# One tile of x moved to GpSimd's queue, and a scratch of its own for the squares, in the opening of an encoder layer

## The chip, the core and the metric

The kernel runs on one core of a Trainium2 chip. A core has five engines that each run their own instruction stream in order: TensorE (PE: matrix products and transposes), VectorE (DVE), ScalarE (ACT), GpSimd (POOL) and SyncE (SP). They wait for one another through semaphores. Transfers between device memory and the on-chip memory are issued by SP, ACT or POOL and carried by 16 DMA engines. The metric is the device time of one execution in microseconds; smaller is better. In this text a "queue" with a q (ACTq, SPq, POOLq) is the part of an engine that issues transfers and handles waits.

## The reference

One layer of a hybrid encoder on 512 positions of width 2048. Cut to what the opening of the kernel computes:

```python
c_act = jax.nn.silu(c)                                # c: one row of 2048
mod = c_act @ w_ada + b_ada                           # 2048 x 6144
shift, scale, gate = jnp.split(mod, 3, axis=-1)
h = rms_norm(x, g) * (1.0 + scale[:, None]) + shift[:, None]
proj = jnp.einsum('bsd,df->bsf', h, w_in)             # 512 x 7168
# attention over three dilated windows and two-way retention on slices of proj,
# gated by silu(z), then
out = jnp.einsum('bsf,fd->bsd', y, w_out)
return x + gate[:, None] * out                        # and a final rms_norm
```

All is float32. The kernel computes each product of two float32 matrices as three products of rounded parts (high by high, high by low, low by high), so that every weight is first split into a high part (ACT) and a low part (DVE).

## The kernel before

**Tiling.** The 512 positions are four tiles of 128 rows (`xn[0]` to `xn[3]`, named `xt` in the profile), each 128 x 2048. The 2048 columns are 16 blocks of 128 (`k`). `h` is kept transposed, one 128 x 512 tile for each block `k`: `hh[k]` the high part, `hl[k]` the low part.

**Two parts of the program.** The projections go over the blocks in chunks of 1, 2, 2, 3, 4 and 4 blocks (`CHUNKS`), because the shift and scale of a block can only be had after a sum over all 2048 rows of `w_ada`. While the matrix products of one chunk run, DVE adds up the rows of `w_ada` for the next (`ada_pieces`: tile `araw` for the raw rows, `aacc` for the sum, three buffers of `araw`, `AR = 3`). The first chunk is block 0 alone, and nothing runs under which its shift and scale could be hidden. It is made in a **prelude** in which TensorE does the sums itself. The prelude is the place of the change. It ends where the first product `pw<-hh,whi` of the projections starts; then come the chunks, the heads and the output projection, which the change leaves as they are.

**The prelude, in the order in which it is written.** For each tile `t` of x: `squares_a(t)` sums the squares of the left half on ACT (tile `sqa`, of which only the sum is used), `squares(t)` those of the right half on DVE (`sqd`); `factor(t)` makes the sum `ms` on DVE and its inverse root `rsx` on POOL; `scaled(t, ...)` multiplies the tile on DVE; `k0_part(t)` and `turned(t, b)` transpose its blocks on PE into `psk` and `psx`; `evacuated(t, b, act)` copies them out on ACT. Between these lie, on PE, `warm(n, ...)` (products whose result is not used, two instructions each), the sums of block 0 `sums0(b, i)` over four transfers `raw0` of `w_ada` (`b`: shift or scale, `i`: upper or lower half of the rows; 512 KB each in pieces of 512 bytes) and `turn_rows()`, which turns the biases and the gain (`bg_row`). `silu_c` makes `ct`, the factors of those sums, from `c_row`.

**What sets the order.** Instructions written through `pin(...)` stay in program order on their engine; the others are placed by a scheduler at build time. An engine's stream is in order at run time: an instruction that waits holds all that stand behind it. Each transfer from SP or ACT is given one of eight completion semaphores in turn (`DMAHW0` to `DMAHW7` in the order listings); the ninth such transfer is issued only after the one that had its semaphore before has landed. Transfers from POOL have semaphores of their own (`DMASW0`, `DMASW1`, ...). Of the prelude's, ACT issues five (four of x, and `raw_w`, the first weights of `w_in`), SP the rest.

**Buffers.** `sqa` is taken from the three buffers of `araw`, so the first three transfers of `araw` have to wait until the squares that use their buffer are done. The prelude's own pool (`xp`) is closed at the end of the prelude, and its room is used again.

Of the kernel before, what the change touches and what calls it, by code (L numbers as in the profile page):

```python
# [9 lines left out]
F32 = mybir.dt.float32  # L10
F32R = mybir.dt.float32r
I32 = mybir.dt.int32
AF = mybir.ActivationFunctionType
# [4 lines left out]
P = 128  # L18
D = 2048
# [13 lines left out]
OFF_QA, OFF_KA, OFF_VA, OFF_ZA = 0, 1024, 2048, 3072  # L33
OFF_QR, OFF_KR, OFF_VR, OFF_ZR = 4096, 4608, 5120, 6144
UC = 256
# [2 lines left out]
ADA_SPAN = 0.65  # L38
TAB_SPAN = 16
WARM = 9, 2, 8, 6, 4  # L40
FIRST_W = OFF_KA + UC
LAG = 3
RAW, RAW1, WB, LOOK, LEAD, LEAD1, EB, YB = 3, 3, 3, 2, 4, 8, 1, 22
GR = 2
# [2 lines left out]
AR = 3  # L47
# [3 lines left out]
def trunk_kernel(ctx, tc, x, c, norm_gain, w_ada, b_ada, w_in, w_out, dec_f, dec_b, final_gain, out):  # L51
    nc = tc.nc
    x2, o2 = x[0], out[0]
    wi, wo, wa = w_in[0], w_out[0], w_ada[0]
# [23 lines left out]
    def raw_tile():  # L78
        early["n"] += 1
        if early["on"] and early["n"] % 2 == 0:  # L80
            return aap.tile([P, 1024], F32, tag="raw1", name="raw1", bufs=RAW1)
        return wp.tile([P, 1024], F32, tag="raw", name="raw", bufs=RAW)
# [12 lines left out]
    c_row = const.tile([NK, P], F32, name="c_row")  # L95
# [9 lines left out]
    aap = xn_scope.enter_context(tc.tile_pool(name="aap", bufs=2, side="right"))  # L105
    x3p = xn_scope.enter_context(tc.tile_pool(name="x3p", bufs=1, side="right"))
    x_scope = ExitStack()
    xp = x_scope.enter_context(tc.tile_pool(name="xp", bufs=1, side="right"))
# [3 lines left out]
    bg_row = const.tile([48, P], F32, name="bg_row")  # L112
    raw0 = [xp.tile([P, NK, P], F32, name=f"raw0{b}") for b in range(2)]
    xn = [(x3p if t == 3 else xp).tile([P, D], F32, name=f"xt{t}") for t in range(NT)]

    def load0(q, b, i):
        q.dma_start(
            raw0[b][:, i * 8 : (i + 1) * 8],
            wa[i * 8 * P : (i + 1) * 8 * P, b * D : b * D + P].rearrange("(a p) f -> p a f", p=P),
        )  # L120

    for q, t, a, b in ((nc.scalar, 0, 0, 1024), (nc.sync, 0, 1024, D), (nc.scalar, 1, 0, D), (nc.scalar, 2, 0, D), (nc.scalar, 3, 0, D)):
        q.dma_start(xn[t][:, a:b], x2[t * P : (t + 1) * P, a:b])
    nc.gpsimd.dma_start(c_row, c.rearrange("b (k p) -> (b k) p", p=P))
    load0(nc.sync, 0, 0)
    load0(nc.sync, 1, 0)

    raw_w = raw_tile()
    nc.scalar.dma_start(raw_w[:, : 2 * UC], wi[0:P, FIRST_W : FIRST_W + 2 * UC])
    load0(nc.sync, 0, 1)  # L130
    load0(nc.sync, 1, 1)
    nc.gpsimd.dma_start(bg_row[0:32, :], b_ada[:, 0 : 2 * D].rearrange("b (k p) -> (b k) p", p=P))
    nc.gpsimd.dma_start(bg_row[32:48, :], norm_gain.rearrange("b (k p) -> (b k) p", p=P))
    ssx = const.tile([P, NT, 2], F32, name="ssx")
    rsx = const.tile([P, NT], F32, name="rsx")

# [6 lines left out]
    nc.gpsimd.memset(mhalf, -0.5)  # L143
    mln2 = const.tile([P, 1], F32, name="mln2")
    nc.gpsimd.memset(mln2, -math.log(2.0))

    ct = const.tile([P, NK], F32, name="ct")
    ce = const.tile([P, NK], F32, name="ce")
# [5 lines left out]
    pin = tc.keep_in_program_order  # L154
    marks = {}
# [155 lines left out]


    def squares_a(t):
        sa = aap.tile([P, 2048], F32, tag="araw", name="sqa", bufs=AR)
        marks["sq"] = pin(nc.scalar.activation(sa[:, 0:1024], xn[t][:, 0:1024], AF.Square, accum_out=ssx[:, t, 0:1]))

    def squares(t):
        sd = aap.tile([P, 1024], F32, tag="aacc", name="sqd")
# [61 lines left out]
    A, B = slice(0, 3 * P), slice(3 * P, S)  # L380
    warm(WARM[0], psk3)
    squares_a(0)
    squares(0)
    factor(0)
# [14 lines left out]
    sums0(0, 0)  # L399
    turn_rows()  # L400
    squares_a(1)
    squares(1)
    factor(1)
# [10 lines left out]
    turned(1, 3)  # L414
    sums0(0, 1)
    squares_a(2)
    squares(2)
    factor(2)
# [122 lines left out]
    def conv(src, n):  # L541
        hi = wp.tile([P, 512], F32R, tag="whi", name="whi", bufs=WB)
        lo = wp.tile([P, 512], F32R, tag="wlo", name="wlo", bufs=WB)
        dh, dl = hi[:, :n], lo[:, :n]
        if len(src.shape) == 3:
            dh = dh.rearrange("p (k f) -> p k f", k=src.shape[1])
            dl = dl.rearrange("p (k f) -> p k f", k=src.shape[1])
        c1 = nc.scalar.copy(dh, src)  # L548
        c2 = nc.vector.tensor_tensor(dl, src, f32(dh), op=ALU.subtract)  # L549
        marks["conv"] = marks.get("conv", 0) + 1  # L550
        if marks["conv"] == 1:
            after(c1, marks["conv1"][0])
            after(c2, marks["conv1"][1])
        elif marks["conv"] < 4:
            after(c1, marks["hh"])
            after(c2, marks["hl"])
        return hi, lo


    def shared_conv(c0s, k0, nk):  # L560
        m = len(c0s)
        lo_c = min(c0s)
        st = {}

        def ld():
            if k0 == 0 and lo_c == FIRST_W:
                assert m == 2
                st["raw"] = raw_w[:, : 2 * UC].rearrange("p (k f) -> p k f", k=1)
            if "raw" not in st:
                raw = raw_tile()  # L570
                rv = raw[:, : nk * m * UC].rearrange("p (k f) -> p k f", k=nk)
                nc.sync.dma_start(
                    rv,
                    wi[k0 * P : (k0 + nk) * P, lo_c : lo_c + m * UC].rearrange("(k p) f -> p k f", p=P),
                )
                st["raw"] = rv

        def cv(j):
            off = (c0s[j] - lo_c) // UC
            if nk == 1:  # L580
                if off // 2 not in st:
                    a, b = off // 2 * 512, min(off // 2 * 512 + 512, m * UC)
                    st[off // 2] = conv(st["raw"][:, 0, a:b], b - a)
                w = st[off // 2]
                o = off % 2 * UC
                return w[0][:, o : o + UC], w[1][:, o : o + UC]
            return conv(st["raw"][:, :, off * UC : (off + 1) * UC], nk * UC)

        return [(ld, lambda j=j: cv(j)) for j in range(m)]
# [310 lines left out]
    k0 = 0  # L900
# [423 lines left out]
```

## Time and profile before

| | us |
|---|---|
| median of 3 runs | 987.12 (985.5 to 988.26) |
| the profiled execution | 985.0 |
| its span, first to last instruction | 983.2 |
| start of the first product of the projections in it | 50.06 |

The profiled execution lies 1.8 us over its span and 2.1 us under the median. Times in the views count from the start of the span. A timeline row gives start, duration, engine, line and operation, and in brackets how long the engine had been idle before and what released it; a row with xN stands for N instructions. A waits row gives total idle time, how often, and the longest. "DMA to landing" is the time from issue to completion of a transfer.

### The profile page before, as it was taken

What the parts mean: (1) busy time and instruction counts of PE and PEld (TensorE: products, weight loads), DVE (VectorE), ACT (ScalarE), POOL (GpSimd) and SP (SyncE); (2) the same over time, 40 slices, a digit from 0 to 9 for tenths busy, and PEclk for the clock granted to TensorE, in tenths of its full rate; (3) what the DMA queues carried; (4) which work ended last, traced back from release to release, by engine and by line L of the source; (5) the groups of instructions that cost most, each with busy time, mean ns of one, the idle gap of its engine ahead of it and who ended that gap; (6) DMA issues with size and microseconds to landing.
All of it is one profiled execution on the core that took longest, in us unless ns stands there. A gap on an engine that the chain in (4) does not pass through costs nothing.

```text
span 983.2 us, 14429 instructions
## 1 busy us (share of the span) xinstructions
PE 948.1 (96%) x5624; PEld 824.5 (84%) x5624; DVE 613.9 (62%) x1076; ACT 376.3 (38%) x738; POOL 12.3 (1%) x25
## 2 busy tenths in 40 slices
PE   3799999999999999999999999999999999999996
PEld 3588688788988888897998899998899988888896
DVE  1499999976968686665655556745534473535444
ACT  1384243425236454454443232432233362323321
POOL 1000000000000000000000000000000000000001
PEclk7899999999999999999999999999999999999998
DMA  9478879733472222222224624526322248234304
GB/s 327 130 256 289 280 233 339 249 125 108 141 224 86 65 65 64 66 65 80 71 65 139 204 87 153 170 65 203 118 65 87 65 154 296 86 110 147 108 1 171
DMA packets 108947, 141.49 MB, mean 144 GB/s; under 512 B 5656, under 2 KB 78024, under 8 KB 108496
## 3 DMA queue, kind: packets, MB, share of 16 engines
q1 hardware_dynamic: 106912, 134.52, 42.2%
q10 hardware_dynamic: 1872, 6.03, 1.6%
q8 instruction: 44, 0.72, 0.3%
q14 instruction: 23, 0.19, 0.1%
q0 software_dynamic: 96, 0.03, 0.0%
HBM read 136.36 MB, written 4.20 MB: 143 GB/s over the span
## 4 chain that ended last, share of the span: by engine, by line
PE 87%; DMA 5%; DVE 4%; issue 2%; ACT 1%; POOL 0%; SPq 0%; POOLq 0%; DVEq 0%; ACTq 0%
PE pp L92 24%; PE pw L92 14%; PE pp L90 12%; PE po L92 12%; PE pw L90 7%; PE po L90 6%; PE op L92 3%; PE sp L92 2%; DMA graw<-in_w_ada_dram 2%; DMA raw<-in_w_ada_dram 2%; PE op L90 2%; PE tp L783 1%; DVE aacc L214 1%; PE sp L90 1%; DMA araw<-in_w_ada_dram 1%
## 5 line engine op out<-in xcount | busy, mean ns | idle before, releaser
L548 ACT CAST whi<-raw 128x512 fp32r<-128x512 f32 (+1 forms) x289 | 175.3, 607 | 432.4 <-PE pp L92 200.9
L549 DVE TENSOR_TENSOR wlo<-raw,whi 128x512 fp32r<-128x512 f32 (+1 forms) x289 | 193.7, 670 | 209.1 <-ACT whi L548 204.7
L92 PE MATMUL pp<-wlo,hh 128*128 128x256 f32 x576 | 161.8, 281 | 0.6 <-DVE wlo L549 0.6
L90 PE MATMUL pp<-whi,hh 128*128 128x256 f32 x576 | 162.3, 282 | 0.0
L92 PE MATMUL pp<-whi,hl 128*128 128x256 f32 x576 | 161.3, 280 | 0.0
L90 PEld LDWEIGHTS pp<-whi,hh 128*128 128x128 f32 x576 | 108.4, 188 | 2.5 <-ACT sc L852 1.7
L92 PEld LDWEIGHTS pp<-wlo,hh 128*128 128x128 f32 x576 | 108.4, 188 | 1.7 <-DVE wlo L549 0.8
L92 PEld LDWEIGHTS pp<-whi,hl 128*128 128x128 f32 x576 | 108.4, 188 | 0.0
L90 PE MATMUL pw<-hh,whi 128*128 128x512 f32 x256 | 102.6, 401 | 1.8 <-DVE acc L955 1.6
L90 PE MATMUL pp<-hh,whi 128*128 128x512 f32 x256 | 102.0, 398 | 0.4 <-DVE kl L683 0.4
L92 PE MATMUL pw<-hh,wlo 128*128 128x512 f32 x256 | 101.4, 397 | 0.0
L92 PE MATMUL pp<-hh,wlo 128*128 128x512 f32 x256 | 101.3, 396 | 0.0
L92 PE MATMUL pw<-hl,whi 128*128 128x512 f32 x256 | 101.1, 395 | 0.0
L92 PE MATMUL pp<-hl,whi 128*128 128x512 f32 x256 | 100.9, 394 | 0.0
L92 PE MATMUL po<-wlo,yh 128*128 128x512 f32 (+1 forms) x252 | 92.6, 367 | 0.0
L92 PE MATMUL po<-whi,yl 128*128 128x512 f32 (+1 forms) x252 | 92.5, 367 | 0.0
L90 PE MATMUL po<-whi,yh 128*128 128x512 f32 (+1 forms) x252 | 92.5, 367 | 0.0
L214 DVE SCALAR_TENSOR_TENSOR aacc<-araw,ct,aacc 128x512 f32<-128x512 f32 (+2 forms) x75 | 76.0, 1013 | 3.6 <-DMA araw<-in_w_ada_dram 2.3
L955 DVE TENSOR_TENSOR acc<-acc,pw 128x512 f32<-128x512 f32 x100 | 66.7, 680 | 8.0 <-PE pw L92 7.5
L1008 DVE SCALAR_TENSOR_TENSOR gacc<-graw,ct,gacc 128x512 f32<-128x512 f32 x60 | 44.9, 749 | 38.5 <-DMA graw<-in_w_ada_dram 38.1
L90 PEld LDWEIGHTS pw<-hh,whi 128*128 128x128 f32 x256 | 48.1, 188 | 16.3 <-DVE acc L955 4.1
L90 PEld LDWEIGHTS pp<-hh,whi 128*128 128x128 f32 x256 | 48.1, 188 | 13.4 <-ACT e L728 0.9
(233 smaller groups left out, 1567.9 us busy)
## 6 DMA issues: line engine op xcount, KB each, us to landing
raw<-in_w_in_dram SPq DMA_DIRECT2D x94, 512.0 KB, 3.7
araw<-in_w_ada_dram SPq DMA_DIRECT2D x48, 512.0 KB, 6.0
graw<-in_w_ada_dram SPq DMA_DIRECT2D x64, 256.0 KB, 2.9
raw<-in_w_out_dram SPq DMA_DIRECT2D x32, 512.0 KB, 3.7
raw<-in_w_in_dram SPq DMA_DIRECT2D x16, 384.0 KB, 3.7
araw<-in_w_ada_dram SPq DMA_DIRECT2D x16, 384.0 KB, 4.8
res<-in_x_dram SPq DMA_DIRECT2D x16, 256.0 KB, 6.7
xt<-in_x_dram ACTq DMA_DIRECT2D x3, 1024.0 KB, 8.1
```

What stands on the lines that cost most here:

```text
L90: nc.tensor.matmul(o, lh, rh, start=start, stop=False, skip_group_check=True)
L92: nc.tensor.matmul(o, a, b, start=False, stop=stop and b is (rl if swap else rh), skip_group_check=True)
L214: ins = nc.vector.scalar_tensor_tensor(acc[:, :, :n], rv[:, a], ct[:, kr + a : kr + a + 1], acc[:, :, :n], op0=ALU.mult, op1=ALU.add,)
L548: c1 = nc.scalar.copy(dh, src)
L549: c2 = nc.vector.tensor_tensor(dl, src, f32(dh), op=ALU.subtract)
L783: nc.tensor.transpose(tp_[:, j * P : (j + 1) * P], pt[:, j * P : (j + 1) * P], ident)
L955: nc.vector.tensor_tensor(accs[u][i], accs[u][i], ps[i], op=ALU.add)
L1008: nc.vector.scalar_tensor_tensor(st["acc"], raw, ct[:, kr : kr + 1], st["acc"], op0=ALU.mult, op1=ALU.add)
```

## The change

Four edits in the prelude:

1. The tile `xn[1]` is issued by POOL, not by ACT. `c_row` stays ahead of it on POOL; the two transfers of `bg_row` go behind POOL's constants.
2. The early transfer `raw_w` on ACT is gone, and with it the special case that used it. These weights are now loaded as all the others are, by SP, behind the four `raw0`.
3. So eight transfers of the prelude are left on SP and ACT (two halves of `xn[0]`, `xn[2]`, `xn[3]`, four `raw0`).
4. `sqa` is a tile of its own in the prelude's pool.

```diff
-FIRST_W = OFF_KA + UC
...
-    for q, t, a, b in ((nc.scalar, 0, 0, 1024), (nc.sync, 0, 1024, D), (nc.scalar, 1, 0, D), (nc.scalar, 2, 0, D), (nc.scalar, 3, 0, D)):
+    nc.gpsimd.dma_start(c_row, c.rearrange("b (k p) -> (b k) p", p=P))
+    for q, t, a, b in ((nc.scalar, 0, 0, 1024), (nc.sync, 0, 1024, D), (nc.gpsimd, 1, 0, D), (nc.scalar, 2, 0, D), (nc.scalar, 3, 0, D)):
         q.dma_start(xn[t][:, a:b], x2[t * P : (t + 1) * P, a:b])
-    nc.gpsimd.dma_start(c_row, c.rearrange("b (k p) -> (b k) p", p=P))
-    load0(nc.sync, 0, 0)
-    load0(nc.sync, 1, 0)
-
-    raw_w = raw_tile()
-    nc.scalar.dma_start(raw_w[:, : 2 * UC], wi[0:P, FIRST_W : FIRST_W + 2 * UC])
-    load0(nc.sync, 0, 1)
-    load0(nc.sync, 1, 1)
-    nc.gpsimd.dma_start(bg_row[0:32, :], b_ada[:, 0 : 2 * D].rearrange("b (k p) -> (b k) p", p=P))
-    nc.gpsimd.dma_start(bg_row[32:48, :], norm_gain.rearrange("b (k p) -> (b k) p", p=P))
+    for i in range(2):
+        for b in range(2):
+            load0(nc.sync, b, i)
...
     nc.gpsimd.memset(mln2, -math.log(2.0))
+
+    nc.gpsimd.dma_start(bg_row[0:32, :], b_ada[:, 0 : 2 * D].rearrange("b (k p) -> (b k) p", p=P))
+    nc.gpsimd.dma_start(bg_row[32:48, :], norm_gain.rearrange("b (k p) -> (b k) p", p=P))
...
     def squares_a(t):
-        sa = aap.tile([P, 2048], F32, tag="araw", name="sqa", bufs=AR)
-        marks["sq"] = pin(nc.scalar.activation(sa[:, 0:1024], xn[t][:, 0:1024], AF.Square, accum_out=ssx[:, t, 0:1]))
+        sa = xp.tile([P, 1024], F32, tag="sqa", name="sqa")
+        marks["sq"] = pin(nc.scalar.activation(sa, xn[t][:, 0:1024], AF.Square, accum_out=ssx[:, t, 0:1]))
...
         def ld():
-            if k0 == 0 and lo_c == FIRST_W:
-                assert m == 2
-                st["raw"] = raw_w[:, : 2 * UC].rearrange("p (k f) -> p k f", k=1)
             if "raw" not in st:
```

How the built program's streams change, at the three places that the prediction speaks of. The semaphore that an instruction waits for stands in brackets; numbers behind a tile's name are buffer numbers, and the change moves the lines by four to seven.

First ACT, from its first transfer to the first copy of transposed blocks. Before:

```order
L123 DMA xt_110<-in_x_dram 128x1024
L123 DMA xt_111<-in_x_dram 128x2048
L123 DMA xt_112<-in_x_dram 128x2048
L123 DMA xt_113<-in_x_dram 128x2048 [waits DMAHW0_49]
L129 DMA raw<-in_w_in_dram 128x512 [waits DMAHW4_49]
L315 ACT_TABLE_LOAD
L315 ACTIVATE sqa,ssx<-xt_110 128x1024
L280 ACTIVATE ce<-ps_149 128x16 [waits PE_49]
L358 COPY xT_93<-psx 128x2x128 [waits PE_49]
```

Now, as far as the squares of the second tile of x:

```order
L123 DMA xt_110<-in_x_dram 128x1024
L123 DMA xt_112<-in_x_dram 128x2048
L123 DMA xt_113<-in_x_dram 128x2048
L311 ACT_TABLE_LOAD
L311 ACTIVATE sqa,ssx<-xt_110 128x1024 [waits DMAHW0_49]
L276 ACTIVATE ce<-ps_147 128x16 [waits PE_49]
L354 COPY xT_93<-psx 128x2x128 [waits PE_49]
L354 COPY xT_94<-psx 128x2x128
L354 COPY xT_95<-psx 128x3x128 [waits PE_49]
L354 COPY xT_96<-psx 128x4x128 [waits PE_49]
L354 COPY xT_97<-psx 128x4x128 [waits PE_49]
L311 ACTIVATE sqa,ssx<-xt_111 128x1024 [waits DMASW1_49,Activation_49]
```

The two transfers that waited for a semaphore are gone from ahead of ACT's table load and squares, and the second tile's squares wait for a semaphore of POOL's transfers.

Then SP, behind the four `raw0` of the prelude. Before:

```order
L117 DMA raw_109<-in_w_ada_dram 128x8x128
L572 DMA raw_385<-in_w_in_dram 128x768 [waits DMAHW1_49]
L572 DMA raw_389<-in_w_in_dram 128x768 [waits DMAHW2_49]
L572 DMA raw_393<-in_w_in_dram 128x256 [waits DMAHW3_49]
L572 DMA raw<-in_w_in_dram 128x768 [waits DMAHW5_49]
L572 DMA raw<-in_w_in_dram 128x256 [waits DMAHW6_49]
L203 DMA araw<-in_w_ada_dram 128x4x256 [waits DMAHW7_49,Activation_49]
L203 DMA araw<-in_w_ada_dram 128x4x256 [waits DMAHW0_49]
L203 DMA araw<-in_w_ada_dram 128x4x256 [waits DMAHW1_49,Activation_49]
L203 DMA araw<-in_w_ada_dram 128x4x256 [waits DMAHW2_49]
L203 DMA araw<-in_w_ada_dram 128x4x256 [waits DMAHW3_49,Activation_49]
```

Now:

```order
L116 DMA raw_109<-in_w_ada_dram 128x8x128
L565 DMA raw<-in_w_in_dram 128x512 [waits DMAHW0_49]
L565 DMA raw_385<-in_w_in_dram 128x768 [waits DMAHW1_49]
L565 DMA raw<-in_w_in_dram 128x768 [waits DMAHW2_49]
L565 DMA raw_389<-in_w_in_dram 128x768 [waits DMAHW3_49]
L565 DMA raw<-in_w_in_dram 128x256 [waits DMAHW4_49]
L565 DMA raw_393<-in_w_in_dram 128x256 [waits DMAHW5_49]
L199 DMA araw<-in_w_ada_dram 128x4x256 [waits DMAHW6_49]
L199 DMA araw<-in_w_ada_dram 128x4x256 [waits DMAHW7_49]
L199 DMA araw<-in_w_ada_dram 128x4x256 [waits DMAHW0_49]
L199 DMA araw<-in_w_ada_dram 128x4x256 [waits DMAHW1_49]
L199 DMA araw<-in_w_ada_dram 128x4x256 [waits DMAHW2_49]
```

The transfer of the first weights (128x512) is new on SP, and the transfers of `araw` no longer wait for ACT.

Last, ACT at the end of the second chunk, where the scheduler places things differently although nothing was edited there (`junk` is the scratch of the sums that give the next chunk's shift and scale, `aacc<-araw` the first step of the sum for the chunk after it). Before:

```order
L548 CAST whi<-raw 128x512 [waits DVE_49,PE_49]
L548 CAST whi<-raw_636 128x512 [waits DMAHW2_49,DVE_49,PE_49]
L210 ACTIVATE aacc<-araw,ct 128x2x384 [waits DMAHW2_49,DMAHW1_49]
L247 ACTIVATE junk,md<-psm 128x128 [waits PE_49]
L247 ACTIVATE junk,md<-psm 128x128
L247 ACTIVATE junk,md<-psm 128x128 [waits PE_49,Activation_49]
L247 ACTIVATE junk,md<-psm 128x128 [waits Activation_49]
```

Now:

```order
L544 CAST whi<-raw 128x512 [waits DVE_49,PE_49]
L243 ACTIVATE junk,md<-psm 128x128 [waits PE_49]
L243 ACTIVATE junk,md<-psm 128x128
L206 ACTIVATE aacc<-araw,ct 128x2x384 [waits DMAHW1_49,DMAHW0_49]
L243 ACTIVATE junk,md<-psm 128x128 [waits PE_49,Activation_49]
L243 ACTIVATE junk,md<-psm 128x128 [waits Activation_49]
L544 CAST whi<-raw_636 128x512 [waits DMAHW3_49,DVE_49,PE_49]
```

Two of the sums stand ahead of the step that waits for a transfer, and a split of weights stands behind it all. On PE the transposes `psm` that feed these sums stand 16 products earlier, and DVE and SP shift a few instructions by one or two places to match.

## The prediction

> **What bounds the kernel now.** I read the page's slices first, then the waits of the first 50 us, then the timeline there. Of section 2 one row matters here, the rate of all transfers in slices of 24.6 us:
>
> ```profile
> GB/s 327 130 256 289 280 233 339 249 125 108 141 224 86 65 65 64 66 65 80 71 65 139 204 87 153 170 65 203 118 65 87 65 154 296 86 110 147 108 1 171
> ```
>
> In the first slice the transfers run at 327 GB/s, in the second, still in the prelude, at 130: something holds them back. The waits of the first 50 us, ACT's and DVE's, and SP's own, name it:
>
> ```profile
> ACT L315 <- DMA raw<-in_w_ada_dram: 17.5, 1, 17.5
> DVE ms L325 <- ACT sqa L315: 14.8, 2, 13.1
> ```
>
> ```profile
> SPq L203 <- ACT sqa L315: 21.0, 3, 8.0
> ```
>
> ACT does nothing for 17.5 us and then is released by a transfer of `w_ada` that it does not read. DVE waits 13.1 us of that for ACT's squares. SP waits 21.0 us for the squares before it issues three loads of `araw`. The timeline shows how the prelude hangs on it:
>
> ```profile
> 0.74 5.47 ACTq L123 DMA_DIRECT2D xt<-in_x_dram  x4
> ...
> 5.68 1.23 DVE L320 CUSTOM_DVE_ANT_0 sqd<-xt 128x1024 f32<-128x1024 f32 x1 [4.80 <-DMA xt<-in_x_dram]
> ...
> 17.18 0.33 ACTq L129 DMA_DIRECT2D raw<-in_w_in_dram  x1
> 17.54 1.28 ACT L315 ACT_TABLE_LOAD   x1 [17.54 <-DMA raw<-in_w_ada_dram]
> 18.84 1.06 ACT L315 ACTIVATE sqa<-xt 128x1024 f32<-128x1024 f32 x1
> 19.80 0.19 ACT L315 ACTIVATION_READ_ACCUMULATOR sqa<-xt 128x1 f32 x1
> ...
> 20.02 0.16 DVE L325 SCALAR_TENSOR_TENSOR ms<-ssx 128x1 f32<-128x1 f32 x1 [13.11 <-ACT sqa L315]
> ...
> 21.87 3.12 PE L347 MATMUL psx<-ident,xt 128*128 128x128 f32 x15
> ...
> 24.82 1.95 PE L378 MATMUL psk<-ident,ones 128*128 128x128 f32 x16
> ...
> 26.70 1.91 PE L296 MATMUL psa<-raw,ct 128*1 128x128 f32 x16
> 28.54 0.26 PE L272 MATMUL ps<-ident,bg_row 48*128 48x48 f32 x1
> 28.84 0.21 DVE L273 COPY bg<-ps 128x48 f32<-128x48 f32 x1 [5.79 <-PE ps L272]
> ...
> 29.16 1.22 DVE L320 CUSTOM_DVE_ANT_0 sqd<-xt 128x1024 f32<-128x1024 f32 x1
> ...
> 32.35 1.73 PE L347 MATMUL psx<-ident,xt 128*128 128x128 f32 x7 [0.21 <-DVE xt L333]
> ...
> 34.01 3.57 PE L296 MATMUL psa<-raw,ct 128*1 128x128 f32 x16
> ...
> 46.33 0.61 ACT L548 CAST whi<-raw 128x512 fp32r<-128x512 f32 x1
> ...
> 49.84 0.73 ACT L210 ACTIVATE aacc<-araw,ct 128x512 f32<-128x512 f32 x1
> ...
> 50.06 0.48 PE L90 MATMUL pw<-hh,whi 128*128 128x512 f32 x1
> ```
>
> ACT issues four loads of x, then the fifth, `raw_w`, at 17.18: it is a ninth or later transfer and stands until an earlier one gives its semaphore back. Behind it stand the table load and the squares, though half of the first tile was there at 5.68 for DVE. From the squares on the prelude is one chain on PE, ACT and DVE, from 18.84 to 50.06.
>
> **The change part by part.** *ACT is free.* With eight transfers on SP and ACT none of ACT's three has to wait. The squares wait for their data alone. When that is there, a narrow window of ACT's timeline tells, for the fourth load of x waited for the first one's semaphore:
>
> ```profile
> 5.88 0.33 ACTq L123 DMA_DIRECT2D xt<-in_x_dram  x1
> ```
>
> So the first half tile has landed by 5.88; the table load (1.28) fits ahead of that. Squares and their readout took from 18.84 to 19.99, 1.15 us: they end at 7.03 instead, just behind DVE's half (6.91). From there to the first sums on PE (26.70) it was 6.71 us of scaling, transposes and warming products; PE would be ready for the sums at 13.74, a gain of 12.96. That is the most that this edit alone can give there.
>
> *What ends last then.* The sums read the first block of `raw0`, issued by SP. Its issue, and the landings of that line (three have a record):
>
> ```profile
> 1.19 0.42 SPq L117 DMA_DIRECT2D raw<-in_w_ada_dram  x1
> ```
>
> ```profile
> DMA to landing us min/median/max: 14.2/15.4/16.7
> ```
>
> The first block lands at 1.19 + 14.2 = 15.39. It is late because the blocks share the DMA engines with x; the queues between 6 and 10 us (packets, MB; q10 is ACT's, q1 SP's, q0 POOL's):
>
> ```profile
> q10 hardware_dynamic: 194, 1.46, 90.9%
> q1 hardware_dynamic: 195, 0.10, 8.8%
> q0 software_dynamic: 87, 0.03, 3.0%
> ```
>
> The queues take turns packet by packet: 194 against 195, but ACT's are of 8 KB (a row of x) and SP's of 512 bytes. So the block gets through only when x is done. The change leaves the bytes of x the same; a third queue takes turns from SP, but x is through no later. I keep 15.39. The bounds: 13.74, where it does not bind, and 17.15, where the second block lands now, if the third queue pushes the first one back by a block:
>
> ```profile
> 1.66 15.49 DMA raw<-in_w_ada_dram
> ```
>
> So the sums start at 15.39 instead of 26.70: **11.3 us** earlier, with bounds of 13.0 and 9.5.
>
> *The rest of the prelude keeps its length.* Behind the sums stands `turn_rows` on PE, behind it the bias copy on DVE, behind that the right half's squares of the second tile (29.16, now 17.85). These need what POOL issues:
>
> ```profile
> 1.26 0.67 POOL L124 DMA_DIRECT2D c_row<-in_c_dram  x1 [0.82 <-POOLq L1313]
> ```
>
> ```profile
> c_row<-in_c_dram POOLq DMA_DIRECT2D x1, 8.0 KB, 5.8
> bg_row<-in_b_ada_dram POOLq DMA_DIRECT2D x1, 16.0 KB, 6.2
> bg_row<-in_norm_gain_dram POOLq DMA_DIRECT2D x1, 8.0 KB, 6.4
> ```
>
> The second tile is issued at 1.93. No row has a megabyte on this queue. From below: 5.8 us as `c_row`, and 1.05 MB at the 1.59 MB in 4 us (397 GB/s) that all queues had together, 2.6 us: 10.4. From above: the same start and a third of that rate, 7.9 us: 15.7. I take 13, since 8 KB packets take turns with ACT's of the same size, half the rate (5.3 us). All lie ahead of 17.85, so the move costs nothing; without that cover each us past it costs one. `bg_row` follows on that queue: 6.4 us from an issue at some 4, or right behind the tile, so by about 16, needed at 28.54 - 11.3 = 17.24. On ACT the wait for the second tile holds the copies of its own transposes, on PE its transposes: both need that tile anyhow. The issue itself, some 0.7 us on POOL as `c_row`'s, trades places with the two of `bg_row`, and POOL's first root is not due before 7.2.
>
> *The first weights move to SP*, behind `raw0`: an issue at about 15.3, up to 2 us of issue, and a landing within about 6.3 us (the median of line L572 to 60 us is 6.2):
>
> ```profile
> DMA to landing us min/median/max: 6.1/6.2/6.3
> ```
>
> That is about 24; their first use at 46.33 becomes 35.0. Hidden. *The scratch of its own* takes SP's 21.0 us of waiting away. The first sum over `araw`, at 49.84, becomes due at 38.5. By 49.2 us the kernel before had moved 24.6 x (327 + 130) = 11.2 MB; at 327 GB/s that takes 34.4 us. The transfers just keep ahead. With the old scratch the third load would have moved with the squares, so this edit is worth nothing alone here, but guards the rest.
>
> *The clock.* The same 16 sums took 1.91 us at 26.70 and 3.57 at 34.01, and the granted clock differs (1.00 and 0.50, the third figure from the right in these rows of two stretches, ahead of the DMA share and the rate):
>
> ```profile
> 26.00:28.00 2.00, 2.00 (x19) 1.59 (x19) 0.00 (x0) 0.66 (x2) 0.00 (x0) 1.00 0.15 8
> 34.00:36.00 2.00, 2.00 (x11) 1.21 (x11) 0.17 (x2) 1.64 (x4) 0.09 (x1) 0.50 0.03 8
> ```
>
> Which stretch falls to half clock may differ after the move; one such group is 1.66 us, either way. I add nothing to the sum and this much to the range. [...]
>
> *After the prelude.* The chunks are bound by DVE, PE and loads that wait for a buffer of `araw`, not by the rate of the transfers: the two long pieces of transfer in the chain, and the rate in two stretches around them,
>
> ```profile
> 86.05 3.73 DMA araw<-in_w_ada_dram
> ...
> 114.55 6.80 DMA araw<-in_w_ada_dram
> ```
>
> ```profile
> 75.00:80.00 5.00, 5.00 (x36) 4.62 (x35) 4.86 (x8) 1.28 (x3) 0.00 (x0) 1.00 1.07 372
> 100.00:110.00 10.00, 10.00 (x45) 8.03 (x44) 10.00 (x15) 1.94 (x4) 0.00 (x0) 1.00 0.70 231
> ```
>
> 231 GB/s before the longer piece, where 372 were to be had: these loads start late, they aren't starved, and so they move with the rest. The scheduler's new order at the second chunk's end puts 16 products less ahead of the transposes `psm`. If their input is late, PE stands still for as long as these products take, at most: by the 45 products in the 10 us of the second row, 16 x 0.22 = 3.6 us. If it isn't, two sums on ACT no longer stand behind the 3.73 us piece. I take nothing, with 2 us either way.
>
> **The sum.** 985.0 - 11.3 = 973.7 us for a profiled execution. The runs' median is 2.1 above that execution, so 987.12 - 11.3 = **975.8 us**.
>
> **The rivals.**
>
> *The gain is half lost.* POOL's tile or `bg_row` lands at 18 to 25 instead of 13, or the new order costs its 3.6 us. For it: each of POOL's tiny transfers took about 6 us. Against: 87 of their 96 packets ran within the 4 us of that row. Price: gain of 3 to 9, 978 to 984.
>
> *More is gained.* The first block lands by 13.74 and the cold stretch at 34.01 runs at full clock: 13.0 + 1.7, and 0.9, half of the 1.73 of the transposes at 32.35: up to 15.6, so 971.5 to 974. Against: nothing moves bytes of x out of the way.
>
> *Only issue time is saved.* [...] As a mechanism here: two of ACT's issues go, 0.33 us each as at 5.88 and 17.18, and its wait reappears at another transfer: 987.12 - 0.7 = 986.4. Against it, in the timeline: between 6.21 and 17.18 ACT issued nothing at all, and now no transfer of ACT waits. A later stage that is fed at a fixed pace would give the same (within 3 us): against it the 231 GB/s.
>
> *Slower.* POOL's queue is starved by the two others, and the second tile lands after 17.85 + 11.3 = 29.2. From there every us is lost; at 35 it would be 987.12 + 5.8 = 992.9. For it: no row shows a large transfer there. Against: 1.05 MB in 27 us would be 39 GB/s, a tenth of the 397 where an even turn would be a third.
>
> **How the numbers follow.** Forecast, gain 8 to 14: 0.60. Half lost: 0.17. More: 0.12. No change: 0.06. Slower: 0.05. The likeliest's own range is 973 to 979; to reach 8 in 10 it takes in most of the half-lost case and some of the larger gain: 972 to 982. Under 0.3% (3 us) a measurement here can't tell a difference. Faster by more: 0.60 + 0.17 + 0.12 = 0.89; same 0.06; slower 0.05.
>
> **What would show it.** ACT's table load near 2 and its first squares near 6; the sums `psa` starting near 15.4, released by `raw0`; the second tile's squares on DVE at or before 18, not waiting for POOL's transfer; the first product `pw` near 38.8; no wait of SP for `sqa`; from there to the end the same 933 us as before. The prediction is wrong if DVE or ACT waits for the second tile, if the sums start past 17.2, or if the stretch from the first `pw` to the end has grown by more than 3 us.

## The result, and the profile after

The changed kernel takes **977.72 us** (median of 4 runs, 974.65 to 979.12) where the kernel before, timed beside it, takes 986.69 (985.5 to 988.26). The ratio is 0.9904, with a 95% interval of 0.9876 to 0.9932: faster by 9.0 us. The profiled execution took 977.17 us, its span is 975.4; before it was 985.0 and 983.2, so 7.8 us less.

First the prelude. These are rows of the timeline of the changed kernel, with the columns as before: start, duration, engine, line, operation, and in brackets the idle time before it and its releaser.

```profile
0.74 1.52 ACTq L123 DMA_DIRECT2D xt<-in_x_dram  x3
1.93 0.56 POOL L123 DMA_DIRECT2D xt<-in_x_dram  x1
2.29 1.28 ACT L311 ACT_TABLE_LOAD   x1 [2.29 <-issue]
5.98 1.06 ACT L311 ACTIVATE sqa<-xt 128x1024 f32<-128x1024 f32 x1 [2.40 <-DMA xt<-in_x_dram]
...
11.17 1.95 PE L374 MATMUL psk<-ident,ones 128*128 128x128 f32 x16
...
12.61 1.06 ACT L311 ACTIVATE sqa<-xt 128x1024 f32<-128x1024 f32 x1 [0.60 <-DMA xt<-in_x_dram]
...
15.47 1.91 PE L292 MATMUL psa<-raw,ct 128*1 128x128 f32 x16 [2.35 <-DMA raw<-in_w_ada_dram]
17.31 0.26 PE L268 MATMUL ps<-ident,bg_row 48*128 48x48 f32 x1
17.93 1.22 DVE L316 CUSTOM_DVE_ANT_0 sqd<-xt 128x1024 f32<-128x1024 f32 x1
...
39.12 0.48 PE L89 MATMUL pw<-hh,whi 128*128 128x512 f32 x1
```

ACT's queue is done with its three loads at 2.26, the table load follows at 2.29 (17.54 before) and the squares at 5.98 (18.84 before), released by their own data. PE has finished its warming products at 13.12 and stands for 2.35 us; then the first block of `raw0` releases the sums at 15.47 (26.70 before). The second tile's squares on DVE run at 17.93 right behind `turn_rows`, without a wait for POOL's transfer. The first product `pw` starts at 39.12 instead of 50.06.

Three of POOL's transfers in the first 20 us, with KB and us from issue to landing:

```profile
xt<-in_x_dram POOLq DMA_DIRECT2D x1, 1024.0 KB, 10.6
...
bg_row<-in_b_ada_dram POOLq DMA_DIRECT2D x1, 16.0 KB, 10.1
bg_row<-in_norm_gain_dram POOLq DMA_DIRECT2D x1, 8.0 KB, 10.3
```

The tile lands at 1.93 + 10.6 = 12.5. ACT stands 0.60 us for it and takes its left half at 12.61; that costs nothing, since ACT then waits 8.5 us for PE's next transposes. DVE takes the right half at 17.93. The two parts of `bg_row`, issued at 3.20 and 3.72, land at 13.3 and 14.0 and are needed at 17.31.

So 11.2 us were won at the sums and 10.9 at the first product. At the end of the span 7.8 are left. The chain of waits between 44 and 82 us shows a place where the loads, not PE, set the time:

```profile
47.11 6.89 DMA araw<-in_w_ada_dram
54.09 0.73 ACT aacc L206
54.84 0.75 DVE aacc L210
55.59 0.07 DVE sv L228
...
69.52 7.67 DMA araw<-in_w_ada_dram
77.28 0.95 ACT aacc L206
78.25 1.02 DVE aacc L210
79.27 0.07 DVE av L246
```

Twice the chain goes from a load of `araw` through the first two steps of a sum (`aacc`, on ACT and on DVE) to a shift or scale (`sv`, `av`). But these steps do not read that sum: `aacc` is here the sum for the chunk after the next, while `sv` and `av` are the shift and scale of the next chunk. They only stand behind the sum in DVE's stream. DVE's own rows at the second place:

```profile
75.30 0.16 DVE L245 TENSOR_TENSOR sv<-md,bg 128x2 f32<-128x2 f32 x1
75.37 0.68 DVE L948 TENSOR_TENSOR acc<-acc,pw 128x512 f32<-128x512 f32 x1
78.25 1.02 DVE L210 SCALAR_TENSOR_TENSOR aacc<-araw,ct,aacc 128x768 f32<-128x768 f32 x1 [2.20 <-ACT aacc L206]
79.19 0.16 DVE L246 TENSOR_TENSOR av<-md,bg 128x2 f32<-128x2 f32 x1
```

DVE waits 2.20 us with `av` right behind. In the kernel before, `sv` and all steps of `av` are done before the first sum of the new group:

```profile
87.98 0.15 DVE L249 TENSOR_TENSOR sv<-md,bg 128x2 f32<-128x2 f32 x1
...
89.14 0.16 DVE L250 TENSOR_TENSOR av<-md,bg 128x2 f32<-128x2 f32 x1 [0.41 <-ACT junk L247]
...
89.81 0.15 DVE L251 TENSOR_TENSOR av<-av,bg 128x2 f32<-128x2 f32 x1
...
91.09 1.01 DVE L214 SCALAR_TENSOR_TENSOR aacc<-araw,ct,aacc 128x768 f32<-128x768 f32 x1
```

To follow where time goes, the span is cut at three rows that every kernel has: the first sums `psa` on PE, the first product `pw` on PE, and the last step of the third scale on DVE (`av<-av,bg 128x3`). Before and after, that last row reads:

```profile
125.64 0.16 DVE L251 TENSOR_TENSOR av<-av,bg 128x3 f32<-128x3 f32 x1
```

```profile
116.54 0.15 DVE L247 TENSOR_TENSOR av<-av,bg 128x3 f32<-128x3 f32 x1
```

| profiled execution (us) | sums | sums to `pw` | `pw` | `pw` to third scale | third scale to end | span |
|---|---|---|---|---|---|---|
| before | 26.70 | 23.36 | 50.06 | 75.58 | 857.56 | 983.2 |
| after | 15.47 | 23.65 | 39.12 | 77.42 | 858.86 | 975.4 |
| difference | -11.23 | +0.29 | -10.94 | +1.84 | +1.30 | -7.8 |

The prelude did what it was to do. Behind `pw` 3.14 us were lost, in two stretches: 1.84 up to the third scale, 1.30 in all that follows.

### The profile page after: what moved, and what is told of

Read it like the earlier page. It is cut to its first block, busy times and chain, and to the rows that moved or that the text cites. A ratio compares the mean times of both kernels' runs of the same rounds, so it can differ in the third digit from the quotient of the medians.

```text
span 975.4 us, 14424 instructions
## 1 busy us (share of the span) xinstructions
PE 948.7 (97%) x5624; PEld 824.8 (85%) x5624; DVE 614.0 (63%) x1076; ACT 376.3 (39%) x738; POOL 12.8 (1%) x26
## 4 chain that ended last, share of the span: by engine, by line
PE 82%; DVE 7%; DMA 7%; issue 2%; ACT 1%; POOL 0%; SPq 0%; POOLq 0%; DVEq 0%; ACTq 0%
PE pp L91 24%; PE po L91 12%; PE pp L89 12%; PE pw L91 12%; PE po L89 6%; PE pw L89 6%; PE op L91 3%; DMA araw<-in_w_ada_dram 3%; DMA graw<-in_w_ada_dram 2%; PE sp L91 2%; DVE aacc L210 2%; PE op L89 2%; DMA raw<-in_w_ada_dram 1%; PE tp L776 1%; DVE acc L948 1%
```

## The experiments

**The theories.** The theory, called A in the expectations: the prelude's gain is the end of ACT's wait at `raw_w`, limited by the landing of `raw0`; and the 1.84 us behind it come from edit 4, the scratch of its own, because with it the scheduler places the new group's sum ahead of the steps of `av`. The rivals: the loss is the clock or chance and not edit 4; GpSimd's queue and the count of eight transfers are needed for the gain; a sum that is held back costs later what it saves. Every experiment is an edit of the changed kernel, except the second, which edits the kernel before. None leaves computation out; the added warming products are extra work whose result is not used. The kernel before was timed in each group of runs and took 986.4 to 987.3 us. All measured values are in the table behind the experiments.

**Edit 4 undone.** The squares go back into the buffers of `araw`:

```diff
-        sa = xp.tile([P, 1024], F32, tag="sqa", name="sqa")
-        marks["sq"] = pin(nc.scalar.activation(sa, xn[t][:, 0:1024], AF.Square, accum_out=ssx[:, t, 0:1]))
+        sa = aap.tile([P, 2048], F32, tag="araw", name="sqa", bufs=AR)
+        marks["sq"] = pin(nc.scalar.activation(sa[:, 0:1024], xn[t][:, 0:1024], AF.Square, accum_out=ssx[:, t, 0:1]))
```

> The changed kernel with edit 4 undone: the squares use a buffer of araw again. In the changed kernel PE ran 10.94 us ahead of the kernel before when the first projection started, but only 8.6 ahead once the third chunk was under way. Theory A (order): edit 4 makes the scheduler put sums that wait for a load of araw ahead of the steps that give the next chunk's shift and scale, on DVE twice (a 256-wide sum and a 384-wide one ahead of the last step) and on ACT once. Without edit 4 DVE's order from the first chunk to the third is that of the kernel before, so the lead stays: 10.9 at the first projection, still 10.5 or more at the 600th product, profiled time about 974 to 975. Theory B (transfers): the lead is lost because the loads of araw come at other times than before, whatever the order; then it is lost here too, the more so as the third load of araw again waits for the squares: lead 8 to 9 at the 600th product, time 977 or more. The prediction's own view, edit 4 guards the rest: the first projection starts up to 3 us later for want of araw.

975.84 us (974.18 to 976.34), ratio 0.9884 (0.9868 to 0.9900). DVE at the start of the third chunk, in its timeline:

```profile
78.64 0.15 DVE L245 TENSOR_TENSOR sv<-md,bg 128x2 f32<-128x2 f32 x1
...
79.80 0.16 DVE L246 TENSOR_TENSOR av<-md,bg 128x2 f32<-128x2 f32 x1 [0.41 <-ACT junk L243]
...
80.47 0.16 DVE L247 TENSOR_TENSOR av<-av,bg 128x2 f32<-128x2 f32 x1
```

The order of the kernel before is back, no sum stands between `sv` and `av`, and from `pw` to the third scale 75.45 us pass (77.42 after, 75.58 before). `pw` itself came at 40.67, 1.55 us later than in the changed kernel. That is the clock and not a want of `araw`: PE's instructions up to `pw` are the same, but half clock fell on the first sums (they took 2.84 us, where the changed kernel took 1.91, and the granted clock was 0.76 from 14 to 18 us and 0.50 from 18 to 22, where it had 1.00 and 0.83), and a later run that keeps the scratch of its own ("The sums held back") has the same late `pw`. The difference of the whole times is too small for the intervals, so it was measured once more, further down.

**Edit 4 alone,** in the kernel before (the same two lines, the other way round):

> The kernel before with edit 4 alone: a scratch of its own for the squares, ACT still held by raw_w. Its order from the first chunk to the third is that of the changed kernel. Theory A (order): the first projection starts as before, within 1.5 us of 50.06, and then 2 us are lost by the 600th product: 987 to 988 profiled, against 985.0 before, some 0.2% slower. Theory B (transfers): the loads of araw come earlier and nothing else moves: no loss behind the first projection, 983.5 to 985.5.

983.63 us (982.32 to 984.85), ratio 0.9965 (0.9952 to 0.9979). The order and its loss come with this edit alone: DVE has the same wait,

```profile
86.12 1.02 DVE L214 SCALAR_TENSOR_TENSOR aacc<-araw,ct,aacc 128x768 f32<-128x768 f32 x1 [1.91 <-ACT aacc L210]
```

and from `pw` to the third scale 77.68 us pass, 2.1 more than before. But the prelude was expected within 1.5 us of the kernel before, and `pw` came 3.7 us earlier, at 46.34. ACT's rows:

```profile
0.74 5.38 ACTq L123 DMA_DIRECT2D xt<-in_x_dram  x4
11.95 0.34 ACTq L129 DMA_DIRECT2D raw<-in_w_in_dram  x1
12.32 1.28 ACT L315 ACT_TABLE_LOAD   x1 [12.32 <-DMA xt<-in_x_dram]
```

`raw_w` is issued at 11.95 instead of 17.18. The built program gives it another completion semaphore to wait for (`DMAHW5` where it was `DMAHW4`). The transfer that had `DMAHW5` is a tile of x, as the last row's releaser says; it lands 5.2 us before the block of `raw0` that had `DMAHW4`. So the place of a scratch tile also moved a wait, through the turn in which semaphores are given out. It confirms the step that the issue of `raw_w` holds ACT, by another route: release it 5.2 us earlier and the squares come 5.2 us earlier (13.62 for 18.84).

**The second tile back on ACT.** `raw_w` stays away, so nine transfers are on SP and ACT instead of eight:

```diff
-    for q, t, a, b in ((nc.scalar, 0, 0, 1024), (nc.sync, 0, 1024, D), (nc.gpsimd, 1, 0, D), (nc.scalar, 2, 0, D), (nc.scalar, 3, 0, D)):
+    for q, t, a, b in ((nc.scalar, 0, 0, 1024), (nc.sync, 0, 1024, D), (nc.scalar, 1, 0, D), (nc.scalar, 2, 0, D), (nc.scalar, 3, 0, D)):
```

> The changed kernel with the second tile of x back on ACT, so that nine transfers of the prelude are on SP and ACT; raw_w stays away from ACT. Theory A (one issue): what held ACT was the issue of raw_w alone, which needed the semaphore of a block of w_ada. The fourth load of x waits only for the first one (landed by 5.9): ACT is free at 6.3, the table load ends at 7.6, squares at 8.8 instead of 7.1; the sums still wait for the first block of raw0 at about 15.4, so nothing is lost: 976.5 to 978, as the changed kernel. Theory B (eight transfers): the ninth transfer brings a wait back that matters, or the third queue is what brings the second tile in time: some us slower than the changed kernel, 980 or more.

976.9 us (975.61 to 977.63), ratio 0.9898 (0.9879 to 0.9917): as good as the changed kernel. ACT and PE:

```profile
0.74 5.42 ACTq L123 DMA_DIRECT2D xt<-in_x_dram  x4
6.19 1.28 ACT L311 ACT_TABLE_LOAD   x1 [6.19 <-DMA xt<-in_x_dram]
...
16.40 1.91 PE L292 MATMUL psa<-raw,ct 128*1 128x128 f32 x16
```

The fourth load of x stands until the first has landed, and the table load comes at 6.19. The sums start at 16.40, now without a wait: PE is the last to arrive, 0.9 us later than `raw0` in the changed kernel. ACT's squares come 1.5 us later (7.49 for 5.98), and part of the 0.9 is that the fifteen transposes ahead of the sums took 3.46 us in one go, where the changed kernel's seven and eight took 0.98 and 1.09; the granted clock reads 1.00 from 10 to 14 us in both, so why they took longer is not shown. So of the 11.2 us at the sums, moving the tile to POOL (edit 1) brings at most 0.9, and taking `raw_w` off ACT (edit 2) the rest; in the whole time the tile's move shows no gain.

**The gaps filled.** In the changed kernel PE falls to half clock twice ahead of `pw` (granted clock 0.50 from 21 to 24 us and from 35 to 37). Warming products are put into the two gaps before that:

```diff
     turn_rows()
+    warm(11, psk3)
...
     turned(2, 1)
+    warm(10, ps0)
```

> The changed kernel with warming products put into two idle stretches of PE in the prelude: 11 (22 instructions, about 2.6 us at full clock) behind the bias transposes, where PE idled from 17.6 to 20.4, and 10 behind the first two banks of the third tile, where it idled from 31.7 to 34.3. They use results of nothing and nothing uses theirs. Theory: the half clock from 20.67 to 24.08 and from 34.32 to 37.73 follows from these idle stretches. Without it 7 transposes and 16 sums take 0.12 us each instead of 0.22 there (about 1.5 us), and the products from 34.3 on 1.6 us less: the first projection at about 36 instead of 39.1, time some 3 us less than the changed kernel, 974 to 975. Rival: the prelude there is held by DVE and ACT, not PE: only the last 1.6 us or nothing is won, and the fill itself may delay PE by up to 0.5 us.

972.82 us (971.79 to 973.73), ratio 0.9856 (0.9840 to 0.9872). PE's rows, and the granted clock in stretches of 4 us (it is the third figure from the right, ahead of the DMA share and the rate), first of this kernel:

```profile
17.59 2.72 PE L374 MATMUL psk<-ident,ones 128*128 128x128 f32 x22
...
36.20 0.48 PE L89 MATMUL pw<-hh,whi 128*128 128x512 f32 x1
```

```profile
18.00:22.00 4.00, 3.43 (x29) 1.00 1.12 342
22.00:26.00 4.00, 4.00 (x36) 1.00 1.06 369
...
34.00:38.00 4.00, 4.00 (x32) 1.00 0.26 76
```

The same stretches of the changed kernel:

```profile
18.00:22.00 4.00, 1.21 (x6) 0.83 1.14 339
22.00:26.00 4.00, 4.00 (x27) 0.74 1.06 371
...
34.00:38.00 4.00, 3.66 (x19) 0.57 0.22 69
```

With the gaps filled the clock stays at full, and from the sums to `pw` 20.63 us pass, where it was 23.36 before and 23.65 after. So half clock costs the changed kernel's prelude about 3 us; that it costs the kernel before as much is likely from its 23.36, but no run here shows it. The loss behind `pw` is there as well (76.59 us), which speaks against the clock as its cause.

**The fourth tile behind `raw0`.** The tile is first read at 30 us, and its bytes go ahead of the `raw0` blocks for which PE waits. SP now issues it behind them:

```diff
-    for q, t, a, b in ((nc.scalar, 0, 0, 1024), (nc.sync, 0, 1024, D), (nc.gpsimd, 1, 0, D), (nc.scalar, 2, 0, D), (nc.scalar, 3, 0, D)):
+    for q, t, a, b in ((nc.scalar, 0, 0, 1024), (nc.sync, 0, 1024, D), (nc.gpsimd, 1, 0, D), (nc.scalar, 2, 0, D)):
...
             load0(nc.sync, b, i)
+    nc.sync.dma_start(xn[3], x2[3 * P : 4 * P, :])
```

> The changed kernel with the last tile of x issued by SP behind the four raw0, not by ACT ahead of them in time. Theory: PE's wait of 2.35 us before the first sums (start 15.47) comes from raw0 standing back behind 4.2 MB of x; with 3.1 MB ahead of it the first block lands some 2.6 us sooner (1.05 MB at 400 GB/s), about 12.8, and the sums start when PE is ready, 13.1 to 13.4. The last tile is needed at 28 and lands by 21. The first projection then starts 2 us sooner, 37 (1.6 us either way by the clock), time 975 to 976. Rival: the blocks of 512-byte pieces are slow by themselves, whatever is ahead: sums still at 15, no gain.

973.13 us (972.21 to 974.65), ratio 0.9868 (0.9855 to 0.9882). The sums on PE:

```profile
12.97 1.91 PE L293 MATMUL psa<-raw,ct 128*1 128x128 f32 x16
```

They start 2.5 us earlier and wait for nothing. What held `raw0` was the x ahead of it, as the prediction had it. Of the 2.5 us 1.4 arrive at `pw` (37.75); the rest goes to a longer stretch at half clock (sums to `pw` 24.78): from 18 to 24 us the granted clock was 0.50, 0.50 and 0.51 in steps of 2 us, where the changed kernel had 1.00, 0.67 and 0.50, and the second group of 16 sums took 3.57 us, for 2.53.

**The sums held back.** The changed kernel, with a rule for the scheduler: in each group the first sum on ACT and on DVE comes behind the steps that make `h`. Cut to its core:

```diff
-                    if k0 == 1:
-                        after(first, marks["hh"])
+                    after(first, marks["hh"] if k0 == 1 else marks["h_act"])
...
-                    if k0 == 1 and kr + a == 1:
-                        after(ins, marks["hl"])
+                    if kr + a == 1:
+                        after(ins, marks["hl"] if k0 == 1 else marks["h_dve"])
```

> The changed kernel with one more rule for the scheduler: the first sum over a new group's araw, on ACT and on DVE, stands behind the steps that make h for the next chunk. Theory A (order): the 2.3 us that the changed kernel lost between the first projection and the 600th product do not appear (its lead of 10.9 stays at 10.5 or more, if the clock falls the same way), and the ACT wait for araw ahead of the third chunk's sums goes too, where PE stood still for some 2.5 us in both kernels: together 3 to 5 us, 973 to 975. Rival: the buffers of araw come free later, the loads start later, and the sums of the next chunk end later by as much: no gain, 977 or more.

976.41 us (975.28 to 978.07), ratio 0.9901 (0.9888 to 0.9915): no different from the changed kernel, where 3 to 5 us were expected. The wait is gone, and with it PE's wait for `wlo` (the low part of a weight). But the first sum of the third group starts on ACT only at 83.91,

```profile
83.91 0.93 ACT L206 ACTIVATE aacc<-araw,ct 128x768 f32<-128x768 f32 x1
```

where it was 77.28 in the changed kernel. So the sums of that group run later, and the stretch takes 75.96 us, 0.5 more than with edit 4 undone. The rival was right in part: something of what is saved is given back. Another part is the clock: from the sums to `pw` this execution took 25.25 us, 1.6 more than the changed kernel, although the rule moves nothing ahead of `pw`; its first sums took 3.19 us, for 1.91, and the granted clock on its page reads 8 tenths in each of the first two of 40 slices, where the changed kernel's reads 9.

**Together.** The two gains (gaps filled, fourth tile behind), once with edit 4 undone and once with the scratch of its own and the sums held back:

> Four things that the runs so far point to, together: the changed kernel with PE's two idle stretches filled, the last tile of x behind raw0, and the squares in a buffer of araw again, so that the order behind the prelude is that of the kernel before. Theory: first projection at 34 to 35 (36.2 with the fill alone, 2 less by the earlier block), the whole lead of some 15.5 us kept to the end: 969.5 to 971.5. If the third load of araw, which waits for the squares again, comes late, some 1 to 2 us of it are lost in the first chunk.

969.09 us (967.76 to 970.2), ratio 0.9825 (0.9812 to 0.9839).

> The same fill and the same place of the last tile of x, with the scratch of its own kept and the order set by the rule of the run on order (first sums of a group behind the steps that make h). Theory: first projection at 34 to 35; if the rule pays as expected, 967 to 970, below the version with the shared buffer; if the later start of the loads takes it back, 971 or more.

968.11 us (967.73 to 968.85), ratio 0.9815 (0.9802 to 0.9829). Both beat the two given kernels, by 17 to 18 us the one before; which of the two is better, the intervals don't tell. Their prelude is 20.64 us from the sums to `pw` in both, and the sums start at 12.95 and 13.20.

**The changed kernel and edit 4 undone, once more,** the two beside each other in five rounds, unchanged:

> The changed kernel as it is, beside its sister with the squares back in the buffers of araw, on one chip. Theory A (the scratch of its own makes DVE's sum stand ahead of the last steps of the scale): DVE waits 1 us or more for ACT's aacc ahead of av at the third chunk's start again, PE stands 0.7 us for wlo once, and from the first product pw to the third scale (av of 128x3) 76.2 to 77.7 us pass, with the whole some 1.5 us slower than the sister. Rival: the 77.42 us were this one profiled execution's, and the second profile shows 75.5, with the whole within 0.7 us of the sister. On the end: if the 858.86 us from the third scale to the end were chance, they are near 857.6 now; if they belong to the kernel, 858.9 again.

> The changed kernel with edit 4 undone, beside the changed kernel on one chip. Theory A: 75.3 to 75.7 us from the first product pw to the third scale, no wait of PE for wlo in that stretch, and a time some 1.5 us below the changed kernel's. Rival: no difference beyond 0.7 us between the two, and a stretch that is as long as the sister's. From the third scale to the end 857.9 us as in its first profile, up to 1 us either way.

976.26 us (974.47 to 977.34, ratio 0.9894, 0.9877 to 0.9911) for the changed kernel, and 975.56 (973.18 to 976.23, ratio 0.9884, 0.9866 to 0.9901) with edit 4 undone. PE's waits between `pw` and the third scale, in total, how often, the longest, first of the changed kernel and then of the other:

```profile
PE pw L89 <- DVE acc L948: 1.7, 2, 1.3
PE psm L238 <- ACT junk L243: 0.7, 1, 0.7
PE pp L91 <- DVE wlo L545: 0.7, 1, 0.7
```

```profile
PE pw L89 <- DVE acc L948: 1.5, 2, 1.3
PE psm L238 <- ACT junk L243: 1.0, 1, 1.0
```

The stretch came out as the theory said, 76.72 against 75.36 us. The whole did not: the difference is 0.7 us where 1.5 were expected, and the intervals overlap. In these two executions the 1.36 us are balanced by the clock: from the sums to `pw` the changed kernel took 23.89 us, the other 25.37, since there the first sums already took 2.95 us, for 1.91 (granted clock 8 tenths in each of the first two of 40 slices, 9 in the changed kernel's). So edit 4 costs 1.4 us in its stretch. The whole times don't show it, since the clock ahead of `pw` varies by as much; the stretch from `pw` to the end does, below the table.

| kernel | median | sums | sums to `pw` | `pw` | `pw` to third scale | third scale to end | span |
|---|---|---|---|---|---|---|---|
| edit 4 undone | 975.84 | 15.31 | 25.36 | 40.67 | 75.45 | 857.88 | 974.0 |
| the same again | 975.56 | 15.47 | 25.37 | 40.84 | 75.36 | 858.20 | 974.4 |
| changed kernel again | 976.26 | 15.69 | 23.89 | 39.58 | 76.72 | 857.70 | 974.0 |
| edit 4 alone | 983.63 | 22.46 | 23.88 | 46.34 | 77.68 | 857.48 | 981.5 |
| second tile on ACT | 976.9 | 16.40 | 23.90 | 40.30 | 76.25 | 857.95 | 974.5 |
| gaps filled | 972.82 | 15.57 | 20.63 | 36.20 | 76.59 | 857.81 | 970.6 |
| fourth tile behind | 973.13 | 12.97 | 24.78 | 37.75 | 75.52 | 859.53 | 972.8 |
| sums held back | 976.41 | 15.44 | 25.25 | 40.69 | 75.96 | 858.55 | 975.2 |
| both gains, edit 4 undone | 969.09 | 12.95 | 20.64 | 33.59 | 74.96 | 857.45 | 966.0 |
| both gains, sums held back | 968.11 | 13.20 | 20.64 | 33.84 | 75.91 | 857.35 | 967.1 |

Read down the column from `pw` to the third scale. The six executions with the changed kernel's order (the changed kernel twice, edit 4 alone, second tile on ACT, gaps filled, fourth tile behind) average 76.70 us; the four with the order of before (before, edit 4 undone twice, both gains with edit 4 undone) 75.34. Each of the six has PE's wait of 0.7 us for `wlo`, none of the four has it. What the order costs beyond that seems to depend on how late the load of `araw` is: with the fourth tile behind, the stretch took 75.52 us, within the range of the four. From `pw` to the end the two groups do not overlap: the six take 934.2 to 936.3 us (934.9 on average), the four 932.4 to 933.6 (933.1). The two with the sums held back take 934.5 and 933.2. So what edit 4 costs, some 1.8 us on average, does reach the end of the kernel. Read down the last stretch: it varies from 857.35 to 859.53 with no clear relation to order or prelude, and for the changed kernel from 858.86 to 857.70 between two executions. Most of the 1.30 us lost there in the first profile did not come back in the second, and so is called chance here; what makes this stretch longer or shorter was not looked into.

## Why the prediction was right, point by point

**ACT is free: right.** Table load at 2.29, squares at 5.98 and done at 7.13 (forecast 7.03). PE would be ready for the sums at 13.12 (forecast 13.74).

**What ends last then: right, and to 0.1 us.** The sums are released by the first block of `raw0` at 15.47 (forecast 15.39); that it would land by 13.74, as the rival "more is gained" had it, did not happen. The queues between 6 and 10 us (packets, MB) show the third one taking an equal turn:

```profile
q10 hardware_dynamic: 107, 0.85, 51.5%
q0 software_dynamic: 112, 0.76, 45.8%
q1 hardware_dynamic: 104, 0.05, 4.5%
```

SP's queue got 104 packets where it had 195, but the block landed when it was forecast to. The experiment with the fourth tile behind `raw0` shows the cause: with 1 MB of x less ahead, the wait is gone. In these 4 us the three queues moved nearly the same number of packets. Those on SP's queue are of 0.05 MB / 104, about 500 bytes, the size of one piece of `raw0`, and two of them most often start 0.64 to 0.66 us apart, the time of one piece and two rows of 8 KB (0.03 + 2 x 0.31 us). So here a turn was one piece.

**POOL's tile and `bg_row`: right.** 12.5 (forecast 13) and 13.3 to 14.0 (forecast by 16). One sign that the prediction had named against itself did come: ACT waited for the second tile, 0.60 us at 12.61. The working had allowed for a wait there ("both need that tile anyhow"), the list of signs had not. It is harmless: ACT is done with its half of the squares at 13.76, DVE with the other half of the same sum only at 19.15. No engine waited for `bg_row`. The rival of a starved queue falls, and so does the half of the rival "half lost" that rested on them.

**Only issue time is saved: wrong as a forecast, and it was given little.** The rival's price was a gain of some 0.7 us; the profile shows 11.2 at the sums. It counted two issues of 0.33 us each. Here one issue cost far more than that: it stood for 11 us (6.21 to 17.18) in ACT's stream with work behind it. Which engine issues the second tile hardly matters (at most 0.9 us with it back on ACT); that ACT issues nothing that has to wait long does.

**The clock: right in kind.** From the sums to `pw` the prelude took 23.36 us before and 23.65 after, a difference of 0.29 inside the 1.66 that were left to the range. That nothing was added was right by luck of where the stretches fell: with the gaps filled, and so without half clock, it takes 20.63, and the changed kernel's instructions on PE took up to 25.37 (edit 4 undone, where the clock fell during the first sums), so this term ranges over 4.7 us, where 1.66 either way is 3.3. The term was sized by one group of 16 sums; half clock stretches over several groups: in the kernel before the granted clock was 0.50 from 32 to 38 us, over seven transposes and 16 sums.

**After the prelude: the term that was mis-sized.** The prediction took "nothing, with 2 us either way", and 933 us from `pw` to the end. It was 936.3 in the first profile, 3.1 more than before and so past the mark of 3 us at which the prediction had called itself wrong, and 934.4 in the second. Two steps stand behind this. The first is the scheduler's new order. The prediction looked at ACT and PE, where "two sums on ACT no longer stand behind the 3.73 us piece", and that came true: `sv` is 36.2 us behind `pw`, 37.9 before. But DVE's stream was not read there; the text ahead of the prediction says that DVE shifts "by one or two places", and this sum moved from the seventh place behind `sv` to the second. There it waited for the same load ahead of `av`, so `av` was 40.1 us behind `pw`, 39.1 before. What was won on ACT was lost on DVE, and the stretch to the third scale grew by 1.8 and 1.1 us in the two profiles. The second is the last stretch, 1.30 and 0.14 us, whose cause stays open.

**The scratch of its own: wrong.** It "is worth nothing alone here, but guards the rest". SP's waits for `sqa` did go, as forecast. But undoing it lost nothing that the clock does not explain, so it guards nothing; it is what changed the order; and alone in the kernel before it brought 3.7 us (983.63 against 987.3), through another semaphore for `raw_w`. The prediction put the new order down to no edit in particular and so had no price for this one.

The sum: 11.23 won at the sums, 0.29 lost to the clock, 1.84 to the order, 1.30 to chance: 7.8 us between the profiled executions, 9.0 between the medians, where 11.3 were forecast. In the second profile the terms are 11.01 - 0.53 - 1.14 - 0.14 = 9.2 us. The forecast of 975.8 us lies 1.9 below the first median and 0.5 below the second, inside the range of 972 to 982.

## What to carry to other kernels

Read an engine's stall at an issue as a stall of all that stands behind it, and look for the transfer whose landing ends it: taking that one issue off the engine was worth 10 to 11 us at the sums, moving a tile of x to another queue hardly anything. When a scheduler places instructions, compare the new streams on every engine that waits for loads, not only where the edit is; a scratch tile in another pool moved a sum ahead of a scale and a wait to another semaphore. And look at what is transferred ahead of the block that ends last, and at idle PE ahead of products at half clock: a tile that was not needed for 15 us yet, and two gaps, were, with the order put right, worth another 7 to 9 us.

## What the runs showed of the hardware

The clock was worth more than expected, and fell behind idle time. In the changed kernel PE was busy for 1.21 of the 4 us from 18 to 22 and got 0.83 and then, from 22 to 26, 0.74 of the clock; with the gap filled, busy for 3.43 us, it got 1.00, and all 20.63 us up to `pw` ran at full clock. The same instructions did not get the same clock in every execution. The changed kernel took 23.65 and 23.89 us from the sums to `pw` in two executions, with a granted clock of 0.83 and 0.96 from 18 to 22 us and of 0.74 and 0.61 from 22 to 26; the same instructions took 25.25 in the run with the sums held back, which differs from it only behind `pw`. The mean granted clock of single executions varied too: it ran from 0.990 to 0.995 in nine of the changed kernel, and over the same range in eight with edit 4 undone.

A megabyte on POOL's queue took 10.6 us from issue to landing beside two other busy queues, and the 16 and 8 KB behind it 10.1 and 10.3, where they took 6.2 and 6.4 in the kernel before: they landed behind it, at 13.3 and 14.0.
